# Normalised residual split bank by bank, FFN operand sums in phases, small gate products placed behind plain ones

## The chip, the core and the metric

The kernel runs on one core of a Trainium2 chip. The metric is the time of one execution in microseconds (us), less is better. Five engines work side by side, each through its own queue in order: PE (TensorE, matrix products), ACT (ScalarE), DVE (VectorE), POOL (GpSimd) and SP (SyncE, which here issues transfers). An instruction that waits holds everything behind it on its engine.

## The reference

One layer of a decoder trunk on 1024 tokens of width 1024, in float32:

```python
u = rmsnorm(h, norm_mix)
# one projection of u: three token mixers and their gates
# A: gated DeltaNet: conv over 4 tokens, silu, l2norm of q and k, per-head decay,
#    a triangular solve in chunks of 64 tokens, then a scan over chunks
# B: mLSTM: running-max stabiliser, matrix memory, chunks of 64
# C: sparse attention: compressed, selected and sliding-window keys
# each branch -> projection -> sigmoid gate; their sum -> output projection
h = h + merged @ w_out
u = rmsnorm(h, norm_ffn)
a, b = split(u @ w_ffn_in)          # 2 x 2816 columns
h = h + (silu(a) * b) @ w_ffn_out
g = sigmoid(rmsnorm(h, norm_ple) @ w_ple_gate)
h = h + (p @ w_ple_proj) * g        # p: 256 values per token
```

The running sums of the decays and of the forget gates, and the running maximum of mixer B, are made for all heads at once ahead of the first head. They are the "gates" of this text.

## The kernel before

Each float32 operand of a large product is split into a high part (`hi`, float32r) and the rest (`lo`), and a product is three matmuls: hi by hi, hi by lo, lo by hi. For the weights ACT makes `whi` from the loaded tile `wraw`, POOL (for some tiles DVE) makes `wlo`. Large products write PSUM tiles named `mm`, 512 columns wide; the program is a list of blocks of four weight tiles each, and `run_blocks` emits them in order. The words "plain matmul" mean those.

**Mixers.** Beside the blocks run generators ("sides"): `gates_side` first, then `gdn_solve(h)` of heads 0 to 3, then mixer B. After each step of a block `advance` lets the sides emit a step or two. `pause(us)` makes a side wait until that much of the program's own count of time, 1.4 for each such step, has gone by. `with self.behind():` ties an instruction behind the last plain matmul emitted; without it a scheduler may put a product among the plain ones where it deems its inputs ready. In `gates_side`, `gcum` is five small products that make all running sums, `mtr` and `mtr2` are transposes that lead to the running maximum, and `msel` picks chunk ends from it. `gdn_solve` makes `kT` and `gq` (conv and silu of k and q, 1024 columns, on DVE and ACT), transposes them (`ktr`), makes `gram` products, solves with many small DVE operations and two trips through memory (`zd`, `xds`), and spreads the result into `gV` (POOL) and `gW` (DVE).

**Norm and FFN.** After the output projection `norm_after` scales a tile of 128 tokens and `to_u2` transposes it, four 128x128 pieces (`u2tr`) to one PSUM bank, and splits each piece: `u2hi` on ACT, `u2lo` on DVE. Work given to `later(lag, ...)` is emitted once the plain products emitted since then add up to that lag in the program's own estimate. The FFN's first pair of column groups is made with seven instead of eight block products, which need sums of the four blocks of u: `ffn_combine(k)` makes for each of four 128-row pieces k the operands T1, T3, T2 and T4 (`uw` the sum, `utT..h` and `utT..l` its parts). Beside that runs `ple_proj_block`: the projection of p, whose 512-column tiles ACT copies out (`pp`). It uses the five `mm` banks in turn. Then come `first_three` (products that need no sum) for two column groups, `last_four` (T2, T3, T1, T4) for both, then `down`. The sums of weights (`ws`) are made on DVE as a block's weights are split.

Of the kernel before, what the change touches and what calls it, by code (L numbers as in the profile page):

```python
# [11 lines left out]
F32 = mybir.dt.float32  # L12
F32R = mybir.dt.float32r
I32 = mybir.dt.int32
AF = mybir.ActivationFunctionType
OP = mybir.AluOpType
AX = mybir.AxisListType

P = 128
# [8 lines left out]
NORM_LAG = 6.0  # L28
# [6 lines left out]
COMBINE_LAG = 8.0  # L35
# [189 lines left out]
class Trunk:  # L225
# [485 lines left out]
    def gates_side(self):  # L711
        nc = self.nc
# [3 lines left out]
        for r in (0, 64):  # L716
            ps = self.ps("gtr")
# [26 lines left out]
        self.beta, self.cg = beta, cg  # L744
        yield

        cum = sm("cum", [P, NT, 8])
        tot = sm("tot", [P, NT, 8])
        gl2 = tmp[:, 64:128]
        ps = self.ps("gcum")  # L750
        for n, m in enumerate((self.tri, self.cross, self.tri128, self.ones, self.rest)):
            self.mm(ps[:, n * 64:n * 64 + 64], m, gl2)
        p8 = ps[:, :320].rearrange("p (n t c) -> p n t c", n=5, c=8)

        nc.vector.tensor_copy(cum[:, :, 0:4], p8[:, 0, :, 0:4])
# [23 lines left out]
        s = sm("m_s", [P, NT, 4])  # L779
        b = cum[:, :, 4:8]  # L780
        nc.vector.tensor_tensor(s, gm[:, :, 12:16], b, OP.subtract)
        ps = self.ps("mtr")
        self.tr(ps[:32, :P], s.rearrange("p t c -> p (t c)"))
        srow = self.b2("m_srow")[:32, :P]
        nc.vector.tensor_copy(srow, ps[:32, :P])
        crow = self.b2("m_crow")[:32, :P]
        nc.vector.tensor_tensor_scan(crow, srow, srow, -3e38, OP.max, OP.max)
        yield from self.pause(2.0)
        ps = self.ps("mtr2")
        with self.behind():  # L790
            self.tr(ps[:, :32], crow)
# [3 lines left out]
        ps = self.ps("msel")  # L795
# [1042 lines left out]
    def norm_after(self, tt, which):  # L1838
        nc = self.nc
        h = self.h[tt]  # L1840
        sq = self.small("na_ssq", [P, 2], bufs=3)
        xn = [self.l2("xn") for _ in range(2)]
        for s in range(2):
            nc.scalar.activation(xn[s], h[s], AF.Square, scale=D ** -0.5, accum_out=sq[:, s:s + 1])
        ms = self.small("na_ms", [P, 1], bufs=3)
        nc.vector.scalar_tensor_tensor(ms, sq[:, 0:1], EPS, sq[:, 1:2], OP.add, OP.add)
        r, c = self.rsqrt_col(ms, "na")
        for s in range(2):
            nc.vector.tensor_scalar(xn[s], h[s], r, c, OP.mult, OP.mult)  # L1849
        self.later(NORM_LAG, lambda: self.to_u2(tt, which, xn))  # L1850
        if which == "ffn" and tt == NT - 1:
            self.ub = {n: [None] * 4 for n in ("T1", "T2", "T3", "T4")}
            self.ub["B11"], self.ub["B21"] = ([self.u2["ffn", k + 4 * j, 0] for k in range(4)] for j in range(2))
            for k in range(4):
                self.later(NORM_LAG + COMBINE_LAG * k, lambda k=k: self.ffn_combine(k))

    def to_u2(self, tt, which, xn):
        nc = self.nc

        hf, q = tt // 4, tt % 4  # L1860
        if q == 0:
            for kc in range(KC):
                self.u2[which, kc, hf] = (self.l2("u2hi", F32R), self.l2("u2lo", F32R))
        gain = self.chan[which]
        for s in range(2):
            ps = self.ps("u2tr")
            for k in range(4):
                self.tr(ps[:, k * P:k * P + P], xn[s][:, k * P:k * P + P])
            for k in range(4):
                kc = 4 * s + k  # L1870
                hi, lo = self.u2[which, kc, hf]
                self.split(hi[:, q * P:q * P + P], lo[:, q * P:q * P + P], ps[:, k * P:k * P + P], gain[:, kc:kc + 1])

    def u2c(self, kc, hf):
        return self.u2["ffn", kc, hf]
# [3 lines left out]
        s = slice((tt % 4) * P, (tt % 4) * P + P)  # L1879
        return hi[:, s], lo[:, s]  # L1880

    def ffn_combine(self, k):


        nc = self.nc
        B = lambda k, hf: self.u2["ffn", k, hf]
        def part(n, t, pool=None):
            hi, lo = self.l2("ut" + n + "h", F32R, pool), self.l2("ut" + n + "l", F32R, pool)
            nc.scalar.activation(hi, t, AF.Copy)
            nc.vector.tensor_tensor(lo, t, hi.bitcast(F32), OP.subtract)  # L1890
            self.ub[n][k] = hi, lo

        def whole(pair):
            t = self.l2("uw")
            nc.vector.tensor_tensor(t, pair[0].bitcast(F32), pair[1].bitcast(F32), OP.add)
            return t

        b12, b22 = whole(B(k, 1)), whole(B(k + 4, 1))
        t1 = whole(B(k, 0))
        nc.vector.tensor_tensor(t1, b12, t1, OP.subtract)  # L1900
        part("T1", t1, self.late2)
        nc.vector.tensor_tensor(b12, b22, b12, OP.subtract)
        part("T3", b12)
        nc.vector.tensor_tensor(b22, b22, t1, OP.subtract)
        part("T2", b22, self.late2)
        t4 = whole(B(k + 4, 0))
        nc.vector.tensor_tensor(t4, t4, b22, OP.subtract)
        part("T4", t4)

    def ffn_blocks(self):  # L1910

# [315 lines left out]
```

## Time and profile before

| | |
|---|---|
| median of 3 runs | 2344.22 us (2343.32 to 2344.37) |
| the profiled execution, and its span | 2347.51 us, 2345.7 us |
| busy: PE, DVE, ACT, POOL | 96%, 57%, 36%, 31% of the span |
| mean granted clock of PE | 0.988 of full |
| chain that ended last | PE 81%, DVE 10%, issue 4%, ACT 2% |

A row of the timeline gives start, duration, engine, line, operation, output and inputs, count, and in brackets how long the engine had been idle before it and what released it. Matmuls overlap, so the spacing of starts tells their rate. A clock of 1.0 is 2.4 GHz; the other level is 1.2 GHz.

### The profile page before, as it was taken

What the parts mean: (1) busy time and instruction counts of PE and PEld (TensorE: products, weight loads), DVE (VectorE), ACT (ScalarE), POOL (GpSimd) and SP (SyncE); (2) the same over time, 40 slices, a digit from 0 to 9 for tenths busy, and PEclk for the clock granted to TensorE, in tenths of its full rate; (3) what the DMA queues carried; (4) which work ended last, traced back from release to release, by engine and by line L of the source; (5) the groups of instructions that cost most, each with busy time, mean ns of one, the idle gap of its engine ahead of it and who ended that gap; (6) DMA issues with size and microseconds to landing.
All of it is one profiled execution on the core that took longest, in us unless ns stands there. A gap on an engine that the chain in (4) does not pass through costs nothing.

```text
span 2345.7 us, 32721 instructions
## 1 busy us (share of the span) xinstructions
PE 2263.3 (96%) x12008; PEld 1794.0 (76%) x12008; DVE 1339.0 (57%) x3071; ACT 855.2 (36%) x1824; POOL 736.0 (31%) x621
## 2 busy tenths in 40 slices
PE   8999999999999999999999999979999999999999
PEld 6777777888688986666667777757888888888877
DVE  5536565624134439888852565676555555555584
ACT  5323242323222435555543224452222222222362
POOL 1442433332211223222111422223444443444412
PEclk9999999999999999999999999989999999999999
DMA  3121211211302232111116524321111111111134
GB/s 131 68 66 68 76 64 47 84 41 60 99 28 82 82 117 69 50 48 40 41 41 229 187 101 157 116 108 57 48 54 50 54 50 50 50 54 54 54 120 146
DMA packets 115833, 184.16 MB, mean 79 GB/s; under 512 B 24603, under 2 KB 34628, under 8 KB 115672
## 3 DMA queue, kind: packets, MB, share of 16 engines
q1 hardware_dynamic: 115240, 181.76, 22.8%
q8 instruction: 95, 1.56, 0.3%
q14 instruction: 66, 0.54, 0.1%
q10 hardware_dynamic: 432, 0.30, 0.0%
HBM read 150.25 MB, written 31.76 MB: 78 GB/s over the span
## 4 chain that ended last, share of the span: by engine, by line
PE 81%; DVE 10%; issue 4%; ACT 2%; DMA 1%; POOL 1%; SPq 0%; DVEq 0%; ACTq 0%; POOLq 0%
PE mm L241 66%; PE nso L241 3%; PE ptr L249 2%; PE S L241 2%; DVE P L1592 1%; PE mops L241 1%; POOL wlo L433 1%; PE gks L241 1%; PE gram L241 1%; DVE kT L891 1%; PE gpu L241 1%; DVE P L1581 1%; DVE xn L1849 0%; DVE u2lo L319 0%; DVE rsq_tna L307 0%
## 5 line engine op out<-in xcount | busy, mean ns | idle before, releaser
L433 POOL TENSOR_TENSOR wlo<-wraw,whi 128x512 fp32r<-128x512 f32 x332 | 442.9, 1339 | 992.8 <-ACT whi L431 768.9
L241 PE MATMUL mm<-u,whi 128*128 128x512 f32 x1856 | 622.9, 409 | 2.0 <-ACT mg L1721 2.0
L431 ACT ACTIVATE whi<-wraw 128x512 fp32r<-128x512 f32 x404 | 253.5, 630 | 431.6 <-PE mm L241 338.4
L241 PEld LDWEIGHTS mm<-u,whi 128*128 128x128 f32 x1856 | 341.3, 191 | 73.2 <-issue 5.2
L241 PE MATMUL mm<-u,wlo 128*128 128x512 f32 x928 | 375.4, 405 | 4.6 <-POOL wlo L433 4.6
L241 PEld LDWEIGHTS mm<-u,wlo 128*128 128x128 f32 x928 | 176.7, 190 | 42.9 <-POOL wlo L433 5.4
L1956 DVE TENSOR_TENSOR fc<-fc,mm 128x512 f32<-128x512 f32 x152 | 103.2, 686 | 156.6 <-PE mm L241 156.4
L2061 DVE TENSOR_TENSOR xt<-xt,mm 128x512 f32<-128x512 f32 x176 | 118.6, 685 | 60.5 <-PE mm L241 59.2
L433 POOL TENSOR_TENSOR wlo<-ws,whi 128x512 fp32r<-128x512 f32 x66 | 92.9, 1408 | 173.4 <-ACT whi L431 170.6
L241 PE MATMUL mm<-whi,alo 128*128 128x512 f32 x352 | 140.8, 400 | 0.0
L241 PE MATMUL mm<-whi,ahi 128*128 128x512 f32 x352 | 139.7, 397 | 0.8 <-ACT ahi L1921 0.8
L241 PE MATMUL mm<-wlo,ahi 128*128 128x512 f32 x352 | 139.6, 397 | 0.0
L1587 ACT ACTIVATE P<-P,n_ng 128x640 f32<-128x640 f32 (+7 forms) x128 | 92.8, 727 | 54.1 <-DVE n_ng L1585 53.6
L433 DVE TENSOR_TENSOR wlo<-wraw,whi 128x512 fp32r<-128x512 f32 x72 | 66.1, 918 | 74.9 <-ACT whi L431 74.4
L431 ACT ACTIVATE whi<-ws 128x512 fp32r<-128x512 f32 x66 | 41.5, 629 | 179.6 <-DVE xt L2061 128.5
L241 PE MATMUL mm<-u2hi,wlo 128*128 128x512 f32 x264 | 104.0, 394 | 0.9 <-POOL wlo L433 0.9
L241 PE MATMUL mm<-u2hi,whi 128*128 128x512 f32 x264 | 104.5, 396 | 0.1
L241 PE MATMUL mm<-u2lo,whi 128*128 128x512 f32 x264 | 104.5, 396 | 0.0
L249 PE MATMUL ptr<-ident,P 128*128 128x128 f32 x528 | 88.1, 280 | 8.2 <-DVE P L1592 7.5
L241 PE MATMUL mm<-whi,u 128*128 128x256 f32 x512 | 94.3, 283 | 0.0
L249 PEld LDWEIGHTS ptr<-ident,P 128*128 128x128 f32 x528 | 60.5, 140 | 40.0 <-DVE P L1592 13.2
L241 PEld LDWEIGHTS mm<-whi,alo 128*128 128x128 f32 x352 | 66.3, 188 | 18.9 <-DVE alo L1922 3.4
(518 smaller groups left out, 4779.4 us busy)
## 6 DMA issues: line engine op xcount, KB each, us to landing
wraw<-in_w_dram SPq DMA_DIRECT2D x412, 256.0 KB, 2.4
mgs<-mg SPq DMA_DIRECT2D x48, 256.0 KB, 2.1
mgld<-mgs SPq DMA_DIRECT2D x48, 256.0 KB, 5.7
xt<-in_x_dram SPq DMA_DIRECT2D x8, 512.0 KB, 7.7
xt<-in_x_dram SPq DMA_DIRECT2D x16, 256.0 KB, 5.5
pps<-pp SPq DMA_DIRECT2D x16, 256.0 KB, 2.9
pg<-pps SPq DMA_DIRECT2D x16, 256.0 KB, 3.8
out_dram<-sg SPq DMA_DIRECT2D x15, 256.0 KB, 2.6
```

What stands on the lines that cost most here:

```text
L241: return self.nc.tensor.matmul(out, lhsT, rhs, start=start, stop=stop).ins
L249: self.nc.tensor.transpose(out, in_, self.ident[:n, :n])
L431: nc.scalar.activation(hi, t, AF.Copy)
L433: eng.tensor_tensor(lo, t, hi.bitcast(F32), OP.subtract)
L891: nc.vector.scalar_tensor_tensor(y, xs[:, k:k + S], w[:, k:k + 1], y, OP.mult, OP.add)
L1581: nc.vector.tensor_tensor_reduce(pt[:, farw:nk], sp2[:, farw - cut:nk - cut], near[g][:, n % 2], 1.0, -3e38, OP.add, OP.max, mx[:, n, 1:2])
L1587: nc.scalar.activation(pts[i][:, :nk], pts[i][:, :nk], AF.Exp, bias=ng[:, i:i + 1], accum_out=sm[:, g, i % 2:i % 2 + 1])
L1592: nc.vector.tensor_scalar(pts[i][:, :nk], pts[i][:, :nk], sm[:, g, i % 2:i % 2 + 1], gate[:, g, i % 2:i % 2 + 1], OP.mult, OP.mult)
L1956: nc.vector.tensor_tensor(t, x, ps, OP.add)
L2061: nc.vector.tensor_tensor(self.h[tt][s], self.h[tt][s], ps, OP.add)
```

## The change

Three edits. In `to_u2` the four high parts of a bank are issued first, then the four low parts. `ffn_combine` is called sixteen times, by operand first and piece second, each operand with a lag of its own; the sums `uw` are kept between the calls. In `gates_side` a pause of 3 stands ahead of `gcum` and of `mtr`, the one ahead of `mtr2` is 5 instead of 2, and `gcum` and `mtr` are tied behind the last plain matmul.

```diff
+        yield from self.pause(3.0)
         cum = sm("cum", [P, NT, 8])
...
-            self.mm(ps[:, n * 64:n * 64 + 64], m, gl2)
+            with self.behind():
+                self.mm(ps[:, n * 64:n * 64 + 64], m, gl2)
...
+        yield from self.pause(3.0)
         ps = self.ps("mtr")
-        self.tr(ps[:32, :P], s.rearrange("p t c -> p (t c)"))
+        with self.behind():
+            self.tr(ps[:32, :P], s.rearrange("p t c -> p (t c)"))
...
-        yield from self.pause(2.0)
+        yield from self.pause(5.0)
         ps = self.ps("mtr2")
...
-            for k in range(4):
-                self.later(NORM_LAG + COMBINE_LAG * k, lambda k=k: self.ffn_combine(k))
+            self.uw = [None] * 4
+            for n, at, lag in (("T2", 8.0, 4.0), ("T1", 24.0, 1.0), ("T3", 28.0, 1.0), ("T4", 32.0, 0.8)):
+                for k in range(4):
+                    self.later(at + lag * k, lambda n=n, k=k: self.ffn_combine(n, k))
...
+            for k in range(4):
+                kc = 4 * s + k
+                nc.scalar.activation(self.u2[which, kc, hf][0][:, c], ps[:, k * P:k * P + P], AF.Copy,
+                                     scale=gain[:, kc:kc + 1])
             for k in range(4):
                 kc = 4 * s + k
                 hi, lo = self.u2[which, kc, hf]
-                self.split(hi[:, q * P:q * P + P], lo[:, q * P:q * P + P], ps[:, k * P:k * P + P], gain[:, kc:kc + 1])
+                nc.vector.scalar_tensor_tensor(lo[:, c], ps[:, k * P:k * P + P], gain[:, kc:kc + 1],
+                                               hi[:, c].bitcast(F32), OP.mult, OP.subtract)
...
-    def ffn_combine(self, k):
+    def ffn_combine(self, n, k):
...
+        if n == "T2":
+            b12, b22, t1 = whole(k, 1), whole(k + 4, 1), whole(k, 0)
+            nc.vector.tensor_tensor(t1, b12, t1, OP.subtract)
+            nc.vector.tensor_tensor(b12, b22, b12, OP.subtract)
+            nc.vector.tensor_tensor(b22, b22, t1, OP.subtract)
+            self.uw[k] = {"T1": t1, "T2": b22, "T3": b12}
+            part(b22, self.late2)
+        elif n == "T4":
+            t4 = whole(k + 4, 0)
+            nc.vector.tensor_tensor(t4, t4, self.uw[k]["T2"], OP.subtract)
+            part(t4)
+        else:
+            part(self.uw[k][n], self.late2 if n == "T1" else None)
```

On PE, at the gates, the order before was this (`g_tmp` holds the gate logarithms, `m_s` is the input of the running maximum, a row with x2 is two matmuls):

```order
62 L241 MATMUL mm<-u,wlo 128x512
63 L241 MATMUL gcum<-g_tmp,cset 128x64 x3
64 L241 MATMUL gcum<-g_tmp,c_129 128x64
65 L241 MATMUL gcum<-g_tmp,cset 128x64
66 L241 MATMUL mm<-u,whi 128x512 x2
67 L241 MATMUL mm<-u,wlo 128x512
68 L241 MATMUL mm<-u,whi 128x512 x2
69 L241 MATMUL mm<-u,wlo 128x512
70 L249 MATMUL mtr<-ident,m_s 32x128
71 L241 MATMUL mm<-u,whi 128x512 x2
```

After the change the same engine has 18 more plain matmuls ahead of `gcum`, and between `gcum` and `mtr` it has 24 (rows 78 to 93, of which the first two and the last two pairs stand here):

```order
74 L241 MATMUL mm<-u,wlo 128x512
75 L241 MATMUL gcum<-g_tmp,cset 128x64 x3
76 L241 MATMUL gcum<-g_tmp,c_129 128x64
77 L241 MATMUL gcum<-g_tmp,cset 128x64
78 L241 MATMUL mm<-u,whi 128x512 x2
79 L241 MATMUL mm<-u,wlo 128x512
92 L241 MATMUL mm<-u,whi 128x512 x2
93 L241 MATMUL mm<-u,wlo 128x512
94 L249 MATMUL mtr<-ident,m_s 32x128
```

Counted over all plain matmuls, `gcum` moves from the 86th to the 104th, `mtr` from the 92nd to the 128th, the first `ktr` of head 0 from the 182nd to the 224th and its third, which needs `gq`, from the 194th to the 236th. All later small products of mixers A and B stand 36 plain matmuls later, until the orders meet again at the 1952nd.

On ACT, at the end of the norm, the order before was this:

```order
955 L318 ACTIVATE u2hi<-u2tr,chan 128x128 [waits PE_49]
956 L318 ACTIVATE u2hi<-u2tr,chan 128x128 [waits DVE_49] x4
957 L1889 ACTIVATE utT1h<-uw 128x512 [waits DVE_49]
958 L1889 ACTIVATE utT3h<-uw 128x512 [waits DMAHW5_49,DVE_49]
959 L1889 ACTIVATE utT2h<-uw 128x512 [waits DVE_49]
960 L1889 ACTIVATE utT4h<-uw 128x512 [waits DVE_49]
961 L2110 ACTIVATE pp<-mm 128x512 x2
962 L2110 ACTIVATE pp<-mm 128x512 [waits DMAHW2_49,Activation_49]
```

And this is the same place after the change:

```order
941 L1878 ACTIVATE u2hi<-u2tr,chan 128x128 [waits PE_49]
942 L1878 ACTIVATE u2hi<-u2tr,chan 128x128 x3
943 L2126 ACTIVATE pp<-mm 128x512 x2
944 L2126 ACTIVATE pp<-mm 128x512 [waits DVE_49,PE_49] x2
945 L1902 ACTIVATE utT2h<-uw 128x512 [waits DVE_49]
946 L2126 ACTIVATE pp<-mm 128x512 [waits PE_49,Activation_49]
947 L2126 ACTIVATE pp<-mm 128x512 [waits PE_49]
```

A high part now waits for PE alone, once a bank, and one `utT2h` stands where four operands of a piece stood ahead of the copies `pp`.

On POOL, in the second block of weights that stands beside head 0's solve, the order before was this (1198 to 1210 are the four `wlo` tiles of head 1's first block, used by the 370th, 376th, 382nd and 388th plain matmul):

```order
L433 TENSOR_TENSOR wlo_1198<-wraw_1070,whi_1197 128x512
L433 TENSOR_TENSOR wlo_1202<-wraw_1072,whi_1201 128x512
L433 TENSOR_TENSOR wlo_1206<-wraw_1074,whi_1205 128x512
L1013 TENSOR_TENSOR gV_1178<-zd_1120,c128_129 128x512
L433 TENSOR_TENSOR wlo_1210<-wraw_1076,whi_1209 128x512
L433 TENSOR_TENSOR wlo_1278<-wraw_1213,whi_1277 128x512
```

After the change 1135 to 1147 are those four, and 1278 to 1290 those of the next block, used by the 466th to the 484th:

```order
L433 TENSOR_TENSOR wlo_1143<-wraw_1049,whi_1142 128x512
L433 TENSOR_TENSOR wlo_1147<-wraw_1051,whi_1146 128x512
L433 TENSOR_TENSOR wlo_1278<-wraw_1150,whi_1277 128x512
L1017 TENSOR_TENSOR gV_1252<-zd_1191,c128_129 128x512
L433 TENSOR_TENSOR wlo_1282<-wraw_1152,whi_1281 128x512
```

`gV` has moved behind all four tiles of the first of the two blocks, and ahead of the second tile of the next. In head 2 it moves the other way round a block: the `wlo` used by the 1102nd matmul now stands behind `gV`, where before it was the one used by the 1096th.

## Rows read from the trace of the kernel before

**Rows 1.** Windows: busy us and count by engine, granted clock, DMA share, GB/s.

```profile
42.00:60.00 18.00, 13.65 (x65) 10.01 (x64) 9.18 (x30) 7.03 (x15) 4.96 (x5) 0.81 0.00 1
...
1500.00:1600.00 100.00, 79.40 (x335) 61.83 (x334) 76.40 (x148) 51.73 (x107) 25.14 (x19) 0.90 0.29 105
1600.00:2250.00 650.00, 649.22 (x2791) 520.21 (x2790) 367.66 (x551) 191.47 (x346) 256.06 (x192) 1.00 0.15 51
```

**Rows 2.** Waits of PE: waiting, awaited, us in total, times, longest.

```profile
PE mm L241 <- ACT pp L2110: 9.4, 1, 9.4
...
PE mm L241 <- POOL wlo L433: 7.1, 8, 3.5
PE mm L241 <- ACT whi L431: 5.8, 1, 5.8
...
PE u2tr L249 <- DVE u2lo L319: 3.2, 3, 1.4
PE ktr L249 <- DVE gq L894: 3.2, 1, 3.2
PE ptr L249 <- DVE u2lo L319: 2.2, 1, 2.2
...
PE gcum L241 <- issue: 1.9, 1, 1.9
...
PE mtr L249 <- DVE m_s L781: 1.6, 1, 1.6
```

**Rows 3.** Timeline of PE at the gates, 44 to 56 us.

```profile
44.43 0.63 PE L241 MATMUL mm<-u,whi 128*128 128x512 f32 x2
44.90 0.40 PE L241 MATMUL mm<-u,wlo 128*128 128x512 f32 x1
47.17 0.85 PE L241 MATMUL gcum<-g_tmp,cset 128*128 128x64 f32 x6 [1.88 <-issue]
...
48.28 1.04 PE L241 MATMUL mm<-u,whi 128*128 128x512 f32 x2
49.11 0.63 PE L241 MATMUL mm<-u,wlo 128*128 128x512 f32 x1
...
54.93 0.57 PE L241 MATMUL mm<-u,wlo 128*128 128x512 f32 x1
```

**Rows 4.** Timeline of DVE, convs of head 0.

```profile
71.13 1.09 DVE L889 TENSOR_SCALAR kT<-xk,chan 128x1024 f32<-128x1024 f32 x1 [5.98 <-ACT xk L876]
...
85.19 1.22 DVE L894 SCALAR_TENSOR_TENSOR gq<-ct,gq 128x1024 f32<-128x1024 f32 x1 [1.12 <-ACT ct L893]
```

**Rows 5.** Timeline of POOL at head 0's solve.

```profile
139.23 1.04 POOL L1013 TENSOR_TENSOR gV<-zd,c 128x512 f32<-128x512 f32 x1 [6.24 <-DMA zd<-xds]
```

**Rows 6.** Timeline of PE at the same place.

```profile
141.99 0.80 PE L241 MATMUL mm<-u,wlo 128*128 128x512 f32 x1 [3.47 <-POOL wlo L433]
```

**Rows 7.** Timeline of ACT, end of the norm.

```profile
1511.38 0.37 ACT L318 ACTIVATE u2hi<-u2tr,chan 128x128 fp32r<-128x128 f32 x1 [0.42 <-DVE u2lo L319]
...
1523.61 2.46 ACT L318 ACTIVATE u2hi<-u2tr,chan 128x128 fp32r<-128x128 f32 x8 [1.99 <-PE u2tr L249]
...
1534.61 0.63 ACT L1889 ACTIVATE utT4h<-uw 128x512 fp32r<-128x512 f32 x1 [1.78 <-DVE uw L1907]
1535.15 2.53 ACT L2110 ACTIVATE pp<-mm 128x512 f32<-128x512 f32 x5
```

**Rows 8.** Timeline of PE behind the norm.

```profile
1535.78 0.80 PE L241 MATMUL mm<-whi,pThi 128*128 128x512 f32 x1 [9.43 <-ACT pp L2110]
...
1539.36 0.63 PE L241 MATMUL mm<-whi,pTlo 128*128 128x512 f32 x1
```

**Rows 9.** Timeline of DVE in the FFN's start.

```profile
1553.68 1.37 DVE L1890 TENSOR_TENSOR utT1l<-uw,utT1h 128x512 fp32r<-128x512 f32 x1 [5.37 <-ACT utT1h L1889]
1554.97 0.68 DVE L1904 TENSOR_TENSOR uw<-uw 128x512 f32<-128x512 f32 x1
```

**Rows 10.** Timeline of POOL at the same time.

```profile
1553.20 1.30 POOL L433 TENSOR_TENSOR wlo<-wraw,whi 128x512 fp32r<-128x512 f32 x1 [1.06 <-ACT whi L431]
```

More of the change, by code (lines that the diff above doesn't have):

```diff
@@ L1868, in to_u2 @@
                 self.tr(ps[:, k * P:k * P + P], xn[s][:, k * P:k * P + P])
+            c = slice(q * P, q * P + P)
+            for k in range(4):
+                kc = 4 * s + k
+                nc.scalar.activation(self.u2[which, kc, hf][0][:, c], ps[:, k * P:k * P + P], AF.Copy,
+                                     scale=gain[:, kc:kc + 1])
             for k in range(4):
@@ L1880, in u2t, with part @@
         return hi[:, s], lo[:, s]
-    def ffn_combine(self, k):
+    def ffn_combine(self, n, k):
         nc = self.nc
-        B = lambda k, hf: self.u2["ffn", k, hf]
-        def part(n, t, pool=None):
+        def part(t, pool=None):
             hi, lo = self.l2("ut" + n + "h", F32R, pool), self.l2("ut" + n + "l", F32R, pool)
@@ L1891, in part, with whole @@
             self.ub[n][k] = hi, lo
-        def whole(pair):
+        def whole(c, hf):
             t = self.l2("uw")
-            nc.vector.tensor_tensor(t, pair[0].bitcast(F32), pair[1].bitcast(F32), OP.add)
-            return t
[L1898 to L1908, printed above, removed]
+            hi, lo = self.u2["ffn", c, hf]
+            nc.vector.tensor_tensor(t, hi.bitcast(F32), lo.bitcast(F32), OP.add)
+            return t
+        if n == "T2":
[11 more added lines that the diff above has]
+            part(self.uw[k][n], self.late2 if n == "T1" else None)
     def ffn_blocks(self):
```

## The prediction

> **What bounds the kernel now.** I read the windows first. From 1600 to 2250 us PE is busy 649.22 of 650 us at full clock, and most of the span is like that: what is saved ahead of such a stretch reaches the end of the run, as long as weights arrive (the DMA engines are busy 0.15 there). Two windows are not like that: 42 to 60 us, with PE busy 13.65 of 18 us at a granted clock of 0.81, and 1500 to 1600 us, with 79.40 of 100 us at 0.90 [rows 1]. Then I read what PE waits for [rows 2]. The longest wait is one of 9.4 us for ACT's copies `pp`; the next are 5.8 us for a `whi`, 3.5 us (of 7.1) for a `wlo`, 3.2 us for `gq`, 2.2 us for `u2lo`, 1.9 us ahead of `gcum`, 1.6 us for `m_s`. The stages that the change touches hold all of these. Last comes what a wait costs beyond its own length. Before `gcum` two plain matmuls take 0.47 us from start to start, behind its wait two take 0.83 us [rows 3]: 0.235 and 0.415 us each, the 2.4 and the 1.2 GHz level. I take 0.18 us for every matmul that runs at the lower level.
>
> **Gates.** `gcum` waits 1.88 us and `mtr` 1.6 us [rows 2, 3]. From 48.28 to 54.93 us stand 12 plain matmuls at the lower level [rows 3], so 12 x 0.18 = 2.2 us. Together 5.7 us. After the change 18 more plain matmuls (4.2 us) stand ahead of `gcum`, against a wait of 1.9, and 24 (5.6 us) between it and `mtr`. Before, 6 stood there, at the lower level (6 x 0.415 = 2.5 us), and the wait of 1.6: DVE needs some 4.1 us from `gcum` to `m_s`, and the new cover exceeds that by 1.5 us. I take the 5.7 us whole; if this cover fails, `mtr` keeps at worst its 1.6 us, so the bounds are 4.1 and 5.7.
>
> **What is 36 matmuls later.** The two transposes of `gq` wait 3.2 us [rows 2], and four matmuls behind that run at the lower level, 0.7 us: 3.9 us. DVE begins the two convs at 71.13 us, after 5.98 us in which it waited for ACT's copy `xk`, and ends them at 86.41 us [rows 4]. After the change ACT has `xk` ahead of the `decay` exponentials, for which it waited, and PE comes to the third `ktr` 42 plain matmuls (9.8 us) later in its own order. The sum of both is more than 3.2 us, but DVE now has the running maximum's small operations beside the convs. I take 3.5 us, bounds 0 and 3.9 (5.7 if waits of about 1 us on `wlo` and `kT` near it go as well, which I don't count).
> Next is `wlo` behind `gV`. POOL waits 6.24 us for a transfer before `gV`, and the `wlo` queued behind it holds PE for 3.47 us [rows 5, 6], after which 12 plain matmuls run at the lower level, 2.2 us: 5.7 us. After the change `gV` stands ahead of a tile that is used at the 472nd matmul. Before, PE stopped at the 388th matmul, at 138.5 us, and `gV` ended at 140.3 us, as long as 8 matmuls later: at the 396th, which in the order is 112 behind the second `gram` of head 0 (the 284th). After the change that `gram` is at the 326th; 326 + 112 = 438, and the 34 up to the 472nd are 8 us of cover. I take 5.7 us, bounds 0 and 5.7. In head 2 the same sum is 998 + 112 = 1110 against a use at the 1102nd: up to 8 matmuls (1.9 us) and a `wlo` of 1.3 us, 3.2 us, that was not there before. Small products of another head stand among the plain ones there, however, and stretch the time that these take; I take 0.6 us of loss, bounds 0 and 5.4 (3.2, and 2.2 for the clock).
> The chains being 8.4 us later costs nothing in itself: the orders meet again at the 1952nd plain matmul, with plain work left beside all of them.
>
> **Norm.** Each `u2hi` waits for the `u2lo` of the piece before: 0.37 us of work behind 0.42 us of waiting, 0.79 us a piece, 3.2 us a bank [rows 7]. Back to back eight take 2.46 us, 0.31 each [rows 7]; so the high parts of a bank take 1.2 us, and the four low parts (bounded by as much) follow while ACT makes the next bank. Of the 2.2 us (`ptr`) and the 1.4 us (`u2tr`) that PE waits for banks here, I estimate that 2.7 us remain, since the first banks still stand among ACT's `whi`.
>
> **FFN operands.** Before, ACT waits 1.78 us for the last sum of the first piece, makes `utT4h` at 1534.61 and only then the copies at 1535.15; PE had stopped for 9.43 us with all five banks full [rows 7, 8]. After it, ACT has a pair of copies ahead of every `utT2h`, and a group of five banks holds 30 matmuls, 7 us of PE's work, while the sums of one T2 are seven DVE operations of 0.68 us, 4.8 us [rows 9]. So the stop of 9.4 us goes. I leave 1.2 us of it, for the first three copies now stand behind 16 high parts (5 us).
> The lower level holds 8 matmuls behind the wait of 1.4 us, 9 from 1535.78 to 1539.36 us [rows 8] and 9 behind the wait for `whi`: 26 x 0.18 = 4.7 us. The wait of 5.8 us for that `whi` came of `ws`, made on DVE after all sixteen operands; now the order has the sums of weights of the first `last_four` ahead of T4. What is late next is the second `last_four`: its `ws` stand behind T4, and its first product needs two sums (1.4 us), a `whi` (0.63) and a `wlo` (1.3 us, [rows 10]): I put down 3.3 us, and 0.7 us for T4 itself and the first `wlo`.
> Sum: 9.4 + 5.8 + 2.2 + 1.4 + 4.7 = 23.5 us now; 2.7 + 1.2 + 3.3 + 0.7 and one stretch of 8 matmuls at the lower level (1.4) = 9.3 us after. Gain 14.2 us, bounds 6 (each remaining wait twice its size) and 23.5.
> One thing could eat it: a DVE operation that begins under a `wlo` takes longer. At 1553.68 us one took 1.37 us, beside a `wlo` from 1553.20 to 1554.50; the next one took 0.68 us [rows 9, 10]. The operands T1 and T3 now lie under the `wlo` tiles of `first_three`. The Trainium skill ("SBUF — State Buffer", section "SBUF: two separate sides") says that VectorE operations with two SBUF inputs and GpSimd operations share a port pair that one holds for its whole instruction while the other is blocked; the row agrees, since the operation ended 0.55 us behind the `wlo`. By rows a hit costs 0.69 us, by that rule up to a whole `wlo`.
>
> **Sum.** 5.7 + 3.5 + 5.7 - 0.6 + 14.2 = 28.5 us. The profiled execution of 2347.5 us becomes 2319.0; it lies 3.3 us over the median, so the median becomes 2315.7 us.
>
> **Rivals.**
> 1. *The FFN's start stays bound by DVE.* The operands are the same sixteen and as many operations; if those behind T2 are hit by four `wlo` on the way to T4, with 4 x 0.69 = 2.8 us, and the second `last_four` waits as long as the first did (5.8 for 3.3, with 9 matmuls at the lower level, 1.6), the gain falls by 2.8 + 2.5 + 1.6 = 6.9 us: 2323 us. For it speaks that DVE is the busiest after PE there, 76.40 us of 100 [rows 1]; against it that most of those were waited for by no one.
> By the rule of the Trainium skill's page a hit is a whole `wlo` of 1.3 us, 5.2 us for four, and the time 2325 us, an estimate.
> 2. *The stops of the heads move and don't go.* `gq` keeps its 3.2 us and head 2 meets the full 5.4: 3.5 + 4.8 = 8.3 us less gain, 2324 us. For it: chains whose length is set by DVE and transfers have cover only by chance of place.
> 3. *Slower: the kept sums wait for stores.* The change keeps twelve sums alive, so the tiles that T2 writes into come from `pp` stores, and its order has DVE wait for a transfer there. If each such wait cost PE a copy (0.5 us), half of what POOL waited for a transfer (3.1 of 6.24 us [rows 5]) and a stretch at the lower level (1.4), 5.0 us, then six would cost 30 us and the change would be worth nothing; from seven on it is slower, 2351 us. Against it: in the order of before DVE has waits for transfers at the same operation too, and none of PE's long waits came of one [rows 2].
> 4. *The reordering of the gates does nothing* because the waits there are as long as the work ahead of them allows: 5.7 us less, 2321 us.
>
> **How the numbers follow.** My forecast 0.55, rival 1 0.17, rival 2 0.12, rival 3 0.06, rival 4 0.06; 0.04 for what I have not seen, either way. The likeliest case gives 2315.7 us, with 2306 to 2324 as its own range (all waits of the FFN gone; the remaining ones half as long again). The range for 8 in 10 reaches to rivals 1, 2 and 4 with some of their sums together: 2304 to 2331 us. A measurement of this kernel tells 0.2%, 4.7 us, from no change: 2339.5 to 2348.9 us is the same. Faster 0.88, the same 0.06, slower 0.06.
>
> **What would show it.** Right: no wait of PE above 2 us for `pp`, for `m_s` or ahead of `gcum`; the window from 42 to 60 us with a clock near 1.0; `u2hi` in fours without waits; the first `down` about 14 us earlier against the end of the norm than before; no wait for a `wlo` near 140 us. Wrong: a wait for `ws` or `whi` of over 6 us at the second `last_four`, DVE operations at 1.3 us and more in a row, a new wait for `wlo` in head 2 near 370 us, or a DVE wait for a transfer ahead of `uw`.

## The result, and the profile after

The changed kernel takes 2325.27 us (median of 4 runs, 2324.71 to 2326.39) against 2343.98 us for the one before (4 runs in turn with them): a ratio of 0.9921 [0.9904, 0.9938], 18.7 us less where 28.5 were forecast. The forecast of 2315.7 us is 9.6 us too low; the time lies 1.3 us above the range of the forecast's own case (2306 to 2324 us) and inside the range for 8 in 10 (2304 to 2331 us). The profiled execution after took 2326.39 us (span 2324.6).

Windows of the kernel after, with the columns of [rows 1]; the second line is 60 to 76 us, where [rows 1] had none:

```profile
42.00:60.00 18.00, 17.50 (x92) 13.87 (x91) 8.76 (x28) 9.40 (x19) 7.28 (x6) 1.00 0.18 58
60.00:76.00 16.00, 12.96 (x45) 9.86 (x44) 15.07 (x21) 2.80 (x4) 11.71 (x8) 0.79 0.05 18
...
1500.00:1600.00 100.00, 90.09 (x364) 68.79 (x363) 85.58 (x134) 43.89 (x90) 26.93 (x18) 0.93 0.29 99
```

The hole at 42 to 60 us is filled (PE 17.50 us busy for 13.65, clock 1.00 for 0.81), but a new one stands right behind it, 12.96 of 16 us at 0.79. The window from 1500 us, which now begins 31 plain matmuls further on in the program, has 10.7 us more of PE, and is still not full.

What PE waits for in the kernel after (awaited, us in total, times, longest):

```profile
PE mm L241 <- ACT whi L431: 4.8, 2, 2.9
PE mytr L249 <- DVE my L1231: 4.2, 1, 4.2
...
PE u2tr L249 <- DVE u2lo L1883: 3.9, 3, 1.7
PE msel L241 <- DVE m_cmx L797: 3.0, 1, 3.0
PE ptr L249 <- DVE u2lo L1883: 2.5, 1, 2.5
PE mm L241 <- POOL wlo L433: 2.4, 7, 0.6
...
PE mm L241 <- ACT pp L2126: 0.8, 2, 0.5
PE mm L241 <- ACT utT4h L1902: 0.8, 1, 0.8
```

Against [rows 2]: `pp` falls from 9.4 to 0.8 us, the longest `wlo` from 3.5 to 0.6, and `gq`, `gcum` and `m_s` are gone. `whi` only falls from 5.8 to 4.8, now in two pieces; `ptr` and `u2tr` did not fall at all; `my` (4.2) and `m_cmx` (3.0) are new.

To see where the time came from I count the plain matmuls (tile `mm`) in both traces and compare the time from one count to another. "Low" is how many of them run at the lower of the clock's two levels (each 0.63 us long instead of 0.40, and 0.43 us from start to start instead of 0.235).

| plain matmuls | before, us (waits, low) | after, us (waits, low) | gain | forecast |
|---|---|---|---|---|
| 72 to 260: gates, convs | 64.7 (9.5, 16) | 56.7 (3.5, 8) | 8.0 | 5.7 + 3.5 |
| 260 to 420: head 0's solve | 49.1 (3.5, 12) | 41.7 (0, 0) | 7.4 | 5.7 |
| 420 to 4300: the other heads, `mytr`, solves | 1287.2 (31.6, 19) | 1287.2 (30.9, 16) | 0.0 | -0.6 |
| 4300 to 4860: norm, FFN's start | 170.8 (22.4, 25) | 164.3 (14.0, 32) | 6.5 | 14.2 |

The four gains make 21.9 us. The two profiled spans differ by 21.1 us; the rest is -1.2 us ahead of the 72nd matmul and 0.3 us behind the 4860th, which the change does not touch, and the pair of profiles lies 2.4 us further apart than the medians. The first three rows together came near their forecast (15.4 of 14.3); the FFN's fell short, by 7.7 us.

### The profile page after: what moved, and what is told of

It reads as the page before. It is cut to its first block, busy times and chain, and to the rows that moved or that the text cites. A ratio compares the mean times of both kernels' runs of the same rounds, so it can differ in the third digit from the quotient of the medians.

```text
span 2324.6 us, 32703 instructions
## 1 busy us (share of the span) xinstructions
PE 2260.6 (97%) x12008; PEld 1790.6 (77%) x12008; DVE 1347.2 (58%) x3071; ACT 851.1 (37%) x1824; POOL 749.9 (32%) x621
## 4 chain that ended last, share of the span: by engine, by line
PE 59%; DVE 8%; issue 4%; DMA 2%; ACT 1%; POOL 1%; SPq 0%; POOLq 0%; DVEq 0%; ACTq 0%
PE mm L241 49%; PE nso L241 3%; PE ptr L249 2%; PE S L241 2%; DVE P L1596 1%; DVE uw L1909 1%; DMA wraw<-in_w_dram 1%; DVE P L1585 1%; POOL wlo L433 1%; PE mops L241 0%; DVE u2lo L1883 0%; PE u2tr L249 0%; PE ncmp L241 0%; DVE n_acc L1644 0%; DVE xn L1853 0%
## 5 line engine op out<-in xcount | busy, mean ns | idle before, releaser
L241 PE MATMUL mm<-u,whi 128*128 128x512 f32 x1856 | 616.5, 407 | 2.0 <-ACT mg L1725 2.0
```

Source lines behind the costliest of these rows:

```text
L241: return self.nc.tensor.matmul(out, lhsT, rhs, start=start, stop=stop).ins
```

## What is late now

**`msel`.** DVE at the running maximum (start, length, operation), kernel after:

```profile
60.15 5.86 DVE L895 SCALAR_TENSOR_TENSOR kT<-xk,chan,kT 128x1024 f32<-128x1024 f32 x3
65.94 1.53 DVE L893 TENSOR_SCALAR gq<-xq,chan 128x1024 f32<-128x1024 f32 x1
67.39 0.18 DVE L797 COPY m_cmx<-mtr 128x32 f32<-128x32 f32 x1
```

and PE at the same place:

```profile
62.98 0.24 PE L249 MATMUL mtr<-ident,m_crow 32*128 32x32 f32 x1
...
67.62 0.64 PE L241 MATMUL msel<-m_cmx,cset 128*128 128x32 f32 x2 [3.04 <-DVE m_cmx L797]
...
70.35 1.05 PE L241 MATMUL mm<-u,whi 128*128 128x512 f32 x2
71.20 0.63 PE L241 MATMUL mm<-u,wlo 128*128 128x512 f32 x1
```

The transpose is done at 63.2 us. Its copy takes 0.18 us, but DVE takes its instructions in order, and the copy stands behind a conv: three operations of 1.95 us and one of 1.53, longer than the 1.22 of [rows 4], while POOL makes `gcb_d` beside them. The copy starts at 67.39, `msel` waits 3.04 us, and behind it two plain matmuls take 0.85 us, the lower level. The longer pause before `mtr2` (5.0 for 2.0) put the transpose beside the conv; before, it was ahead of it.

**`mytr`.** DVE in the short chain that ends in `my`, kernel after:

```profile
652.43 1.17 DVE L1221 TENSOR_TENSOR m_oss<-m_oss,m_rd 128x8 f32<-128x8 f32 x1
653.63 1.31 DVE L1222 TENSOR_TENSOR m_oss<-m_oss,m_rd 128x8 f32<-128x8 f32 x1
...
655.18 1.15 DVE L292 TENSOR_SCALAR rsq_ymo<-m_oss 128x8 int32<-128x8 int32 x1
656.36 0.17 DVE L294 TENSOR_TENSOR rsq_tmo<-rsq_ymo 128x8 f32<-128x8 f32 x1
656.56 1.13 DVE L295 SCALAR_TENSOR_TENSOR rsq_tmo<-rsq_tmo,m_oss 128x8 f32<-128x8 f32 x1
```

and POOL at the same time:

```profile
652.28 5.39 POOL L433 TENSOR_TENSOR wlo<-wraw,whi 128x512 fp32r<-128x512 f32 x4 [3.52 <-ACT whi L431]
```

Operations on 8 elements that take 0.17 us elsewhere in the same chain take 1.13 to 1.31 us, four of them, while POOL makes four `wlo` back to back; behind the last `wlo` every one takes 0.17 us. The four lose 4.1 us together, and PE waits 4.23 us. Before, the same chain ran with no `wlo` beside it, and PE waited 0.16 us, with the same 28 plain matmuls between the last product ahead of the chain and `mytr`. The opposite happened at `gytr`. One of DVE's rows there before, and POOL's beside it:

```profile
204.39 1.30 DVE L295 SCALAR_TENSOR_TENSOR rsq_tgo<-rsq_tgo,g_s 128x8 f32<-128x8 f32 x1
```

```profile
204.37 1.29 POOL L433 TENSOR_TENSOR wlo<-wraw,whi 128x512 fp32r<-128x512 f32 x1 [1.26 <-ACT whi L431]
```

The same operation after:

```profile
201.18 0.17 DVE L295 SCALAR_TENSOR_TENSOR rsq_tgo<-rsq_tgo,g_s 128x8 f32<-128x8 f32 x1
```

Before, four such operations took 1.13 to 1.30 us ahead of the longer of PE's two waits there (3.1 us), and three took 1.15 to 1.27 us ahead of the shorter (2.3 us); after, both waits are gone. The forecast had neither. The change moves these chains by 36 matmuls, and so moves them against POOL's blocks of weights, into one and out of others.

**The FFN's start.** DVE there, kernel after, three rows under POOL's `wlo` tiles and the first behind them:

```profile
1523.78 1.78 DVE L1903 TENSOR_TENSOR utT2l<-uw,utT2h 128x512 fp32r<-128x512 f32 x1
1525.48 1.78 DVE L1914 TENSOR_TENSOR uw<-uw 128x512 f32<-128x512 f32 x1
1527.19 1.77 DVE L1909 TENSOR_TENSOR uw<-u2hi,u2lo 128x512 f32<-128x512 f32 x1
1528.88 0.68 DVE L1915 TENSOR_TENSOR uw<-uw 128x512 f32<-128x512 f32 x1
...
1542.38 0.69 DVE L1988 TENSOR_TENSOR ws<-wraw 128x512 f32<-128x512 f32 x1
...
1560.94 0.68 DVE L1988 TENSOR_TENSOR ws<-wraw 128x512 f32<-128x512 f32 x1
```

POOL beside the first three:

```profile
1523.27 1.75 POOL L433 TENSOR_TENSOR wlo<-ws,whi 128x512 fp32r<-128x512 f32 x1
1525.10 1.61 POOL L433 TENSOR_TENSOR wlo<-wraw,whi 128x512 fp32r<-128x512 f32 x1
```

PE at the first products of the two `last_four`:

```profile
1544.57 0.62 PE L241 MATMUL mm<-utT2h,whi 128*128 128x512 f32 x1 [2.93 <-ACT whi L431]
1544.99 0.63 PE L241 MATMUL mm<-utT2l,whi 128*128 128x512 f32 x1
...
1563.06 0.79 PE L241 MATMUL mm<-utT2h,whi 128*128 128x512 f32 x1 [1.85 <-ACT whi L431]
```

Three things stand in these rows and in the list of waits. The operands themselves are nearly in time: PE waits 0.8 us in all for `pp` and 0.8 us for a `utT4h`. But the sums of weights `ws` for the first `last_four` (1542.38) stand on DVE behind seven of the eight low parts of T1 and T3, those for the second (1560.94) behind all of T4, and each time PE waits for the `whi` made of them, 2.93 and 1.85 us, and for a `wlo`. And behind each wait a run of matmuls has 0.43 us from start to start, from 1544.57 to 1551.48 and from 1563.06 to 1568.48: 25 at the lower level from the 4700th to the 4840th plain matmul, where before had 8.

A hit by a `wlo` costs DVE 1.1 us here, not the 0.69 that I took from one row [rows 9]: with `wlo` tiles back to back the two engines take turns, DVE's starts lie 1.70 us apart and POOL's 1.8, about one `wlo` (1.30 us alone, [rows 10]) and one DVE operation less what overlaps. The Trainium skill ("SBUF — State Buffer", section "SBUF: two separate sides") says of the port pair that the two engines share that whoever starts first holds it for its whole instruction and the other is blocked. These rows agree with that: a turn of 1.7 to 1.8 us for 1.30 and 0.68 us of work, and both engines' records lengthened.

My theory after the result: (A) the gates' part and the FFN's part act apart from each other; in the FFN what is left is the two waits for `whi` and the clock behind them, not the operands; `msel` and `mytr` are accidents of place, which another place takes away. Rivals: (B) the parts depend on each other, the gates' shift spoils the FFN or the other way round; (C) one of the three edits costs time; (D) DVE's total work bounds the FFN's start, so that PE waits as long in whatever order.

## The experiments

Each time is a median, and its ratio is to the kernel before in the same session (2343.8 to 2344.7 us).

### The parts apart

Four kernels, each the kernel before with one part or two. The gates alone, which are the first four pieces of the change's diff:

> Only the gates edit. My theory: the stage of the mixers and the stage behind the norm are independent, and this part is worth what the two traces differ by at the 4300th plain matmul: 12 us faster than before, 2332 us, with the new wait of 3 us ahead of msel and the new one of 4 us ahead of mytr in it. Rival: the chains that stand 36 matmuls later are paid back further on and the gain at the norm is only borrowed: within 5 us of before.

2330.72 us, 0.9941 [0.9924, 0.9958]: -13.5 us. Windows and waits of this kernel:

```profile
42.00:60.00 18.00, 17.50 (x92) 13.83 (x91) 8.74 (x28) 9.41 (x19) 7.25 (x6) 1.00 0.18 58
1500.00:1600.00 100.00, 80.99 (x332) 62.92 (x332) 74.99 (x133) 45.10 (x90) 20.97 (x16) 0.91 0.28 98
```

```profile
PE mm L241 <- ACT pp L2114: 9.4, 1, 9.4
...
PE mm L241 <- ACT whi L431: 5.8, 1, 5.8
...
PE mytr L249 <- DVE my L1231: 4.2, 1, 4.2
```

The first window is that of the whole change, the second that of before with its 9.4 and 5.8 us, and `mytr` is there already: it belongs to the gates' part.

The split alone, bank by bank (the sixth piece):

> Only the four high parts ahead of the four low parts. My theory: the stop of 9.4 us for the copies stays, because they still stand behind four operands of a piece on ACT; what is gained is that DVE starts the sums earlier: 1 to 3 us faster than before, 2341 to 2343 us. Rival: ACT and DVE waiting on each other is what made the sums late, and the stop shrinks by half: 5 us faster or more.

2344.60 us, 1.0006 [0.9996, 1.0017]: nothing. PE still waits 9.1 us in one piece for `pp`, and for `ptr` and `u2tr` 1.7 and 3.9 us where before had 2.2 and 3.2.

The operand sums in phases alone (the fifth and the last piece), and then with the split:

> Only the operands in phases. My theory: this is the part that removes the stop of 9.4 us and gives most of the 6.7 us: 4 to 6 us faster than before, 2338 to 2340 us, with the same two waits at the first products of last_four as the whole change. Rival: without the split the low parts of the last token tile come so late that T2 holds the copies as before: within 2 us of before.

2339.47 us, 0.9980 [0.9970, 0.9989]: -4.7 us.

> The split and the phases without the gates edit. My theory: 6.7 us faster than before, 2337 us, so that this and the gates edit alone add up to the whole change within 2 us. Rival: the parts depend on each other, and the sum differs from 18.7 us by more than 3 us.

2339.32 us, 0.9979 [0.9968, 0.9991]: -4.9 us. The gates' part and this one add up to 18.4 us, the whole change is 18.7. The intervals, 3 to 4 us to either side each, leave room for a few us between these; the traces are sharper. In the first three rows of the table the gates' part alone takes 56.7, 41.7 and 1286.8 us (the change 56.7, 41.7 and 1287.2), and in the last row split and phases take the 164.3 us of the change, with the same 32 at the lower level. Rival B falls. So does C in its plain form: no edit costs time by itself, one is worth nothing that can be measured. Waits of the phases alone:

```profile
PE mm L241 <- ACT whi L431: 4.8, 2, 2.9
...
PE mm L241 <- ACT pp L2116: 2.0, 1, 2.0
```

Without the split the stop for `pp` is already 2.0 us instead of 9.4, and `whi` 4.8 as in the whole change: the phases did all of it.

### The two new waits of the mixers

In the changed kernel the transpose `mtr2` back at its old distance, 12 matmuls earlier:

```diff
-        yield from self.pause(5.0)
+        yield from self.pause(2.0)
         ps = self.ps("mtr2")
```

> The whole change, but the pause ahead of mtr2 is 2 as before. All later small products of the mixers then stand 12 plain matmuls earlier than in the change. My theory: the wait ahead of msel shrinks from 3.0 to 1 or 2 us, since m_cmx now stands behind two of kT's operations and not four; and the waits of gytr and mytr change, because they depend on where the rsqrt's small DVE operations fall against the wlo tiles: some of gytr's 3.1 and 2.3 us come back or mytr's 4.2 us goes. Time 2320 to 2327 us. Rival: gytr and mytr wait by the length of their own chains, and these stay as in the change, with 1.5 to 3 us gained in all, at msel alone.

2318.72 us, 0.9895 [0.9881, 0.9910]: -25.9 us against before, more than the change, though the two intervals overlap by a little. `msel` waits 1.1 us (and `gcb`, new, 0.9 and 0.5 us behind it), and from the 72nd to the 260th plain matmul no matmul runs at the lower level (54.0 us for 56.7). From the 420th to the 4300th the trace has 1280.5 us for 1287.2. `mytr`, which here stands 18 plain matmuls earlier, waits 0.16 us. DVE in its chain, the rows that took 1.17 and 1.15 us after:

```profile
644.38 0.17 DVE L1221 TENSOR_TENSOR m_oss<-m_oss,m_rd 128x8 f32<-128x8 f32 x1
...
644.99 0.17 DVE L292 TENSOR_SCALAR rsq_ymo<-m_oss 128x8 int32<-128x8 int32 x1
```

POOL's next `wlo` begins at 648.37, behind the chain's end at 647.2. To part the two waits, one kernel has `mtr2` at its old distance, covers `msel` by more work, and leaves the chain as late as the change does:

```diff
-        yield from self.pause(5.0)
+        yield from self.pause(2.0)
         ps = self.ps("mtr2")
...
-        yield
+        yield from self.pause(4.0)
         ps = self.ps("msel")
-        self.mm(ps[:, :32], self.sel, cmx.rearrange("p t c -> p (t c)"))
+        with self.behind():
+            self.mm(ps[:, :32], self.sel, cmx.rearrange("p t c -> p (t c)"))
```

> The whole change, with the pause ahead of mtr2 at 2 and one of 4 ahead of msel, which is tied behind a plain matmul. The later small products stand where they stand in the change. My theory: the new wait of 3.0 us ahead of msel (m_cmx stood behind kT's conv on DVE) goes, and the 8 matmuls at the lower level behind it (1.5 us): 4.5 us faster than the change, 2321 us; all waits behind it as in the change. Rival: DVE is the bound there, and what msel no longer waits is waited at gcb or ktr: within 1.5 us of the change.

2318.14 us, 0.9895 [0.9880, 0.9909]. In its trace `msel` does not wait and the stretch takes 51.5 us, but `mytr` waits 4.2 us as in the change. DVE in its chain:

```profile
646.78 1.18 DVE L1222 TENSOR_TENSOR m_oss<-m_oss,m_rd 128x8 f32<-128x8 f32 x1
```

POOL:

```profile
646.63 5.40 POOL L433 TENSOR_TENSOR wlo<-wraw,whi 128x512 fp32r<-128x512 f32 x4 [3.52 <-ACT whi L431]
```

The two waits part: `msel` hangs on the transpose's place against the conv, `mytr` on the chain's place against the four `wlo`. In all six traces that have this chain at the 1952nd plain matmul (the change, the gates alone, and four of the experiments) the same four operations take 1.13 to 1.31 us and `mytr` waits 4.2 us; in the seven others none does and it waits 0.15 to 0.17 us. What covering `msel` alone is worth in time stays open: the median equals that of the earlier chain, but the trace is of an execution of 2323.82 us, and the other three took 2317.2 to 2318.3 us at a mean granted clock of 0.994 to 0.995 for 0.992. The trace has 40 matmuls at the lower level from the 4300th to the 4860th, where the change has 32.

### The FFN's start

Is it the wait for `whi` or the clock behind it? One kernel fills both waits with 10 and 8 matmuls that nothing reads, tied behind the last product of a block:

```diff
-                    self.mm(ps, wl, uh, False, k == 3)
+                    self.last_mm = self.mm(ps, wl, uh, False, k == 3)
...
                 product = products(wb)
+                fill, (fh, _) = self.ps("fill"), self.u2["ffn", 0, 0]
+                with self.behind():
+                    for _ in range((10, 8)[f]):
+                        self.mm(fill, fh[:, :P], fh)
```

> The whole change, with 10 extra matmuls of 512 columns ahead of the first last_four and 8 ahead of the second, whose results nobody reads, in the time in which PE waits there. My theory: the 24 plain matmuls that run at the lower clock level behind these two waits, 4.6 us, are what I forecast too little of; with PE busy through the waits they run at full clock and the time falls by 3 to 5 us, to 2320 to 2322 us. Rival: they are slow for another reason (operands or weights come late), and the extra work gains nothing: 2325 us or 1 us more.

2324.15 us, 0.9920 [0.9904, 0.9937], against 0.9921 for the change: no difference that can be measured. PE there:

```profile
1540.95 2.45 PE L241 MATMUL fill<-u2hi 128*128 128x512 f32 x10
1544.03 0.50 PE L241 MATMUL mm<-utT2h,whi 128*128 128x512 f32 x1 [0.64 <-ACT whi L431]
...
1552.74 0.47 PE L241 MATMUL mm<-utT1h,whi 128*128 128x512 f32 x1 [1.69 <-ACT utT4h L1902]
```

The clock stays up (no matmul at the lower level from the 4700th to the 4840th, for 25), and this stretch takes 45.9 us for 48.2. But PE, faster now, meets a wait of 1.7 us for ACT ahead of T1's product that was not there. ACT at that time:

```profile
1552.07 0.63 ACT L1902 ACTIVATE utT4h<-uw 128x512 fp32r<-128x512 f32 x1 [3.56 <-DVE uw L1921]
```

ACT stands 3.56 us at `utT4h`, waiting for DVE's sum, and PE goes on when that tile is made. It is no operand of T1's product, whose own parts were made by 1541.3 us; what ties the two is not shown. As I read these rows, part of what the clock cost was cover for DVE: D in a milder form.

Are the eight low parts of T1 and T3 in the way? The two phases 5 and 7 steps later, so that `ws` stands ahead of more of them:

```diff
-            for n, at, lag in (("T2", 8.0, 4.0), ("T1", 24.0, 1.0), ("T3", 28.0, 1.0), ("T4", 32.0, 0.8)):
+            for n, at, lag in (("T2", 8.0, 4.0), ("T3", 30.0, 0.8), ("T1", 33.0, 0.8), ("T4", 36.0, 0.8)):
```

> The whole change, with T3 at lag 30 and T1 at 33 in steps of 0.8, and T4 at 36, so that the first sums of weights for last_four stand ahead of most low parts of T1 and T3 on DVE. My theory: the wait of 2.9 us for whi at the first last_four came of those low parts; it goes, with the stretch at the lower level behind it (2.7 us), less up to 2 us of new waits for T3: 2320 to 2323 us. Rival: the low parts are only late in another place, and T3 and T4 wait as much: within 1.5 us of the change.

2322.96 us, 0.9908 [0.9894, 0.9923]. The waits move and don't go, here as PE's list has them:

```profile
PE mm L241 <- ACT utT4h L1902: 3.1, 2, 1.8
...
PE mm L241 <- ACT whi L431: 1.7, 2, 0.9
```

`whi` falls from 4.8 to 1.7 us, so these waits did come of the order on DVE; `utT4h` rises from 0.8 to 3.1. All waits from the 4700th to the 4840th are 8.1 us for 8.0; with 13 matmuls at the lower level for 25 the stretch takes 47.1 us for 48.2. I take from this that DVE's chain as a whole is late here and that its order decides where PE notices; no run shortens the chain, so this is not shown.

If it is so, taking the sums of weights off DVE should help, unless POOL's turns cost more. Three additions to POOL:

```diff
-            nc.vector.tensor_tensor(s1, a21, a22, OP.add)
-            nc.vector.tensor_tensor(s2, s1, a11, OP.subtract)
+            nc.gpsimd.tensor_tensor(s1, a21, a22, OP.add)
+            nc.gpsimd.tensor_tensor(s2, s1, a11, OP.subtract)
...
-            nc.vector.tensor_tensor(a21, a11, a21, OP.subtract)
+            nc.gpsimd.tensor_tensor(a21, a11, a21, OP.subtract)
```

> The whole change, with the three sums of weights of a last_four made on POOL and not on DVE. My theory: DVE's queue (low parts of T1, T3 and T4 ahead of these sums) is why PE waits 2.9 and 1.9 us for whi at the two last_four; on POOL, idle there, the sums come at once, and the stretch from the 4720th to the 4860th plain matmul takes 3 to 6 us less than the 48.2 of the change: 2319 to 2322 us. Rival: the stage is bound by the length of the chain sum, whi, wlo itself, or by the loads of the weights, and POOL's slower sums give nothing: 47 us or more.

2327.53 us, 0.9930 [0.9915, 0.9945]: not faster than the change. POOL in this kernel:

```profile
1537.20 1.74 POOL L1988 TENSOR_TENSOR ws<-wraw 128x512 f32<-128x512 f32 x1
1539.02 1.60 POOL L1989 TENSOR_TENSOR ws<-ws,wraw 128x512 f32<-128x512 f32 x1
```

and DVE beside it:

```profile
1539.41 3.45 DVE L1903 TENSOR_TENSOR utT1l<-uw,utT1h 128x512 fp32r<-128x512 f32 x2
```

A sum costs POOL 1.6 to 1.74 us, and each DVE operation beside it 1.7 us for 0.68: DVE gives up three operations and loses 1.0 us on each of those that run meanwhile. The stretch of 48.2 us (from the 4700th to the 4840th plain matmul; the expectation numbers it 20 higher) takes 51.0 us. The same edit on top of the early `mtr2`:

> The same on the change with a pause of 2 ahead of mtr2. My theory: the two gains are in different stages and add up: 6 us of the one and 3 to 6 of the other, 2313 to 2317 us. Rival for POOL: as without it, 2319 us.

2321.65 us, 0.9907 [0.9891, 0.9924]: again not better than without it (0.9895).

Last, the early `mtr2` and the filling matmuls together:

> The change with a pause of 2 ahead of mtr2, and with the 18 extra matmuls in the two waits. My theory: the extra matmuls are worth the 2.3 us that they saved in their own stretch in the traces before, and in the time as well: 2316 to 2318 us. Rival: what they save is within the scatter, 2319 us.

2317.37 us, 0.9883 [0.9868, 0.9898]: 26.4 us under the kernel before of its session and the fastest of all, though its interval overlaps that of the early `mtr2` alone. Its window from 1500 to 1600 us:

```profile
1500.00:1600.00 100.00, 93.17 (x388) 71.85 (x387) 82.68 (x111) 39.61 (x69) 35.66 (x24) 1.00 0.27 98
```

This trace is of an execution of 2312.90 us; the other three took 2317.3 to 2317.8 us. The window begins further on in the program than that of the change, so its count of matmuls does not compare. From the 4300th to the 4860th plain matmul the trace has 161.9 us with 5 at the lower level, where the change has 164.3 with 32 and before 170.8 with 25.

## Why the prediction was right or wrong, point by point

**Right, by mechanism and size.** The gates: `gcum` and `mtr` no longer wait, the window has clock 1.00, and their part alone gave 13.5 us, where all terms of the mixers together (gates, `gq`, the `wlo` behind `gV`, head 2) were forecast at 14.3. The `wlo` behind `gV`: forecast 5.7, measured 7.4 with no wait and none at the lower level between the 260th and 420th matmul; some 1 us of the 7.4 is 32 small products that now stand behind the 420th. The `gq` wait is gone. The stop of 9.4 us for `pp` is gone, by the phases.

**Right in the sum, wrong in the parts.** Behind the 420th matmul I put down -0.6 us for head 2's `wlo`. That wait did not come. What came was 4.2 us at `mytr` and 2.5 more at `gks` (4.0 for 1.5), and what went was the two `gytr` waits (5.4 us) and some smaller ones. All waits there are 30.9 us for 31.6, 16 matmuls run at the lower level for 19, 32 small products more stand there, and the stretch takes the same 1287.2 us: that the forecast of -0.6 lies near is luck. And `msel` took 3.0 us and 8 matmuls at the lower level (1.4) out of what the gates and `gq` gave. The sentence that failed is "The chains being 8.4 us later costs nothing in itself": I looked at the plain work beside the chains, not at what DVE and POOL do beside them at the new place.

**Wrong in size: the FFN's term.** Forecast 14.2 us, measured 6.5, close to the lower bound of 6. I had the waits fall by 10.9 us (18.8 to 7.9) and the matmuls at the lower level by 18, 3.3 us. All waits of the stretch fell by 8.4 us (22.4 to 14.0), and the matmuls at the lower level rose from 25 to 32, -1.3 us by the same 0.18: 2.5 us are missing in the waits and 4.6 in the clock; 0.6 I can't place. Three steps failed. (1) "Now the order has the sums of weights of the first `last_four` ahead of T4": they are, but behind T1 and T3, and that wait of 2.93 us was in no term; the second `last_four` cost 1.85 us, less than the 3.3 put down. (2) A `wlo` hit costs DVE 1.1 us, not 0.69, and hits three operations in a row behind T2 and more at T4 (1544.92, 1546.72, 1549.99 us). (3) The lower level was counted for one stretch of 8 matmuls where it follows both waits, with 25 matmuls, 3.1 us more. This is the largest of the three, but filling did not bring it back whole: it took 25 matmuls off the lower level, 4.5 us by price, and the stretch became 2.3 us shorter, since another wait, behind DVE's sum for `utT4h`, came next.

**Also wrong: the norm's terms.** Of 3.6 us of waits at `ptr` and `u2tr` 2.7 were to remain; 2.5 and 1.1, the same 3.6 us, did. ACT makes its high parts without waiting, as forecast (twelve in 3.20 us from 1503.29), but PE's waits end with DVE's low parts. The split alone changed the time by nothing.

**Rivals.** 1 (DVE stays the bound of the FFN's start, 2323 us) came nearest: its mechanism is there, DVE hit by `wlo` behind T2, both `last_four` waiting, and its price was 6.9 us against the 7.7 us missing. That the numbers lie so near is in part luck: it had the second `last_four` wait 5.8 us, which was 1.85. It had 0.17, too little. Of my signs of being wrong one came: DVE operations of 1.3 us and more in a row. 2 (stops move) holds in kind, since two moved stops cost 7.3 us, but at other places, and as many went that I had not counted. 3 (kept sums wait for stores) and 4 (the gates' order does nothing) are refuted.

**Open.** How much of the lower clock behind a given wait belongs to the kernel: see below. What holds T1's product behind `utT4h` on ACT is not shown. And whether DVE's chain in the FFN could be shortened rather than re-ordered was not tried.

## What to carry to other kernels

When an edit moves a chain, look at what the other in-order engines do at the new place, not only at whether PE has cover there: here a copy of 0.18 us behind 5.9 us of conv, and operations of 0.17 us beside POOL's splits, cost 7 us of waiting, and 12 matmuls to one side gave 6 us of time back. For each wait that a forecast leaves, write down which instruction of its chain stands where in its engine's queue, and put a price on the slow matmuls behind it. Here re-ordering DVE's chain moved PE's waits and left their sum as it was, and handing three of its operations to POOL, which takes turns with it, gave nothing: the stretch became 2.8 us longer in the trace.

## What the runs showed that I had not expected

The same wait is followed by the lower clock in one run and not in another. `msel` waits 3.0 us in the kernel after and in the one with filling matmuls, which is the same up to there: 8 matmuls at the lower level behind it in the one, none in the other, 56.7 and 54.0 us for the 72nd to the 260th. Between the 4300th and the 4560th, behind a wait of 1.1 us for `u2tr`, the change has 72.6 us and the early `mtr2` 73.6, with 5 more at the lower level. So one profile tells such a place only to 1 to 3 us.

An operation's size does not tell what POOL costs it: on 128x8 elements DVE took 1.13 to 1.31 us beside a `wlo` for 0.17, a loss of 1.0 to 1.1 us, and on 128x512 elements 1.77 for 0.68, the same loss.
